# Two activations of the first feed-forward part in a buffer of their own, and the final norm's factors scaled later

## The chip, the cores and the metric

The kernel runs on one NeuronCore of a Trainium2 chip. Its engines run side by side, each through its own list of instructions: TensorE (PE in the profile) multiplies matrices, VectorE (DVE) and ScalarE (ACT) work on elements, GpSimd (POOL) does a few small things, SyncE (SP) issues transfers from memory. The metric is the device time of one execution in microseconds; smaller is better.

## What is computed

A decoder trunk of two layers over 256 tokens with 1,024 features. Layer 0 mixes tokens with a gated recurrence (HGRN2), layer 1 with attention; a SwiGLU feed-forward part follows each mixer, and a last RMSNorm closes the trunk. Cut to what matters here:

```python
for layer in range(2):
    y = rms_norm(h, norm_mix[layer])
    h = h + (hgrn2_mixer if layer == 0 else moba_mixer)(y, ...)
    h = h + swiglu(rms_norm(h, norm_ffn[layer]), ffn_w13[layer], ffn_w2[layer])
return rms_norm(h, final_norm)

def swiglu(h, w13, w2):              # w13: 1024 x 5632, w2: 2816 x 1024
    g, u = jnp.split(h @ w13, 2, axis=-1)
    return (silu(g) * u) @ w2
```

## The kernel before

**Split products.** Every large product is made of three matmuls, since each float32 operand is split into a high part that TensorE takes and a low part that is the rest: high by high, high by low, low by high. ScalarE makes the high part of a weight tile (`whi`, line 412) and VectorE the low part (`wlo`, line 414) out of the tile `raw` that SyncE has fetched. Six buffers of each kind, of 1,024 columns, follow each other round.

**What is stationary and what moves.** In the mixers' projections and in layer 0's feed-forward part the weights are stationary (128 columns) and the 256 tokens of an activation move past them. The tiles are `xh`/`xl` for a normed input and `hh`/`hl` for the 22 hidden pieces j of a feed-forward part. In the second product of layer 1's feed-forward part it is the other way round: the activation `hh`/`hl` is stationary, and 512 columns of weights move. The helper `mm` (line 455) records all of these.

**A feed-forward part** (`swiglu`) first makes the hidden pieces 0 to 3 together. Then it goes in rounds: for j from 4 to 21 it makes piece j (48 matmuls of 256 columns) and after it applies the second product to piece j-4 (layer 0: 24 matmuls of 256 columns; layer 1: 12 of 512). After the rounds come the last four pieces. `hidden` (line 955 on) turns a finished bank into `hh` and `hl`; ring number `j % 7`, each ring with two buffers that take turns.

**Where the tiles lie.** `lay_out` places the tiles of TensorE's operands first, one after the other in each partition: the weights; a gap of 48 floats (192 bytes); the tiles `x`; then the rings `q1`, `k1`, `q2`, `k2` and so on. The rings `q`/`k` serve the recurrence in layer 0's mixer, and `alias` gives the same memory to `hh`/`hl` later: `hh0` lies in `q1`, `hl0` in `k1`, `hh1` in `q2`. All weight tiles begin at a multiple of 512 bytes, and pieces of them too. Counted from there modulo 256, all `x` tiles and the rings from `q2` on lie at 192 bytes. `q1` and `k1` are different: a gap of 64 bytes goes ahead of them, and their tiles are 48 floats longer than what is used. So their first buffers lie at 0 modulo 256 (256 bytes behind a piece of weights, counted modulo 512), and their second ones at 192. By the turns of the rings, `hh0`/`hl0` are in the first buffers for j = 0 and 14 in layer 0 and for j = 7 and 21 in layer 1.

**Order of the work.** TensorE's order is the program's. For the other engines the class `Order` records each operation with a due time and a cost in nanoseconds, and puts it into its engine's list when its inputs are planned to be ready. On the chip each list then runs strictly in turn: an instruction that waits holds up all behind it.

**The final norm's factors.** Behind layer 1's mixer the kernel needs 1/sqrt of the mean square of each token: squares on ScalarE (`sq`, `sqacc`, line 554 on), their sum on VectorE, eight small matmuls against `ones`, a power on GpSimd (`ny`), and two transposes (line 596). At that place ScalarE also issues the transfer of the 1,024 factors of the last norm into `bt` (line 1136), 512 KB with the copies for all partitions, and multiplies them by a constant (line 1137). They are first read at the end, by GpSimd (line 1182).

Of the kernel before, what the change touches and what calls it, by code (L numbers as in the profile page):

```python
# [8 lines left out]
FT = mybir.dt.float32  # L9
FR = mybir.dt.float32r  # L10
I32 = mybir.dt.int32
U8 = mybir.dt.uint8
AF = mybir.ActivationFunctionType
OP = mybir.AluOpType

P = 128
S = 256
D = 1024
# [264 lines left out]
def cv(n, fast=False):  # L283
    return ((n / 2 if fast else n) + 66) / 0.96


def ca(n, ptr=0):
    return n / 1.2 + 93 + 93 * ptr
# [14 lines left out]
def hybrid_trunk(ctx: ExitStack, tc: tile.TileContext, wts, xT, par, gfin, tab, onehot, masks, out):  # L303
    nc = tc.nc
    V, A, G, T = nc.vector, nc.scalar, nc.gpsimd, nc.tensor

    ctx.enter_context(tc.manual_schedule())
    sb = ctx.enter_context(tc.tile_pool(name="sb", bufs=1))
    ps = ctx.enter_context(tc.tile_pool(name="ps", bufs=4, space=bass.MemoryType.PSUM))
    dr = ctx.enter_context(tc.tile_pool(name="dr", bufs=1, space=bass.MemoryType.DRAM))  # L310
    od = Order()
    rings = {}

    def ring(tag, shape, bufs, dt=FT):
        if tag not in rings:
            rings[tag] = Ring(lambda: sb.tile(shape, dt, name=tag, tag=tag, bufs=bufs), bufs)
        return rings[tag]

    def new(tag, shape, bufs=1, dt=FT, held=False):
        return ring(tag, shape, bufs, dt).new(held)  # L320

    def alias(tag, other, shape, dt=FT):

        o = rings[other]
        wide = [P, S + 48] if other in ("q1", "k1") else shape
        rings[tag] = Ring(lambda: sb.tile(wide, dt, name=tag, tag=other, bufs=o.bufs)[:, :shape[1]], o.bufs)
        rings[tag].past = o.past

    def lay_out():


        sb.tile([P, 96], FT, name="lead")
        for t in ("whi", "wlo"):
            ring(t, [P, SUB], NSUB, FR).make()
        sb.tile([P, 48], FT, name="gap")
        for k in range(KT):
            for part in "hl":
                ring(f"x{part}{k}", [P, S], 2, FR).make()
        for part in "qk":

            sb.tile([P, 16], FT, name=f"gap{part}1")
            rings[f"{part}1"] = Ring(lambda part=part: sb.tile([P, S + 48], FT, name=f"{part}1", tag=f"{part}1",
                                                              bufs=2)[:, :S], 2)
            rings[f"{part}1"].make()
            sb.tile([P, 16], FT, name=f"gap{part}2")
        for m in (2, 4, 8, 16, 32, 64):
            for part in "qk":
                ring(f"{part}{m}", [P, S], 2).make()

    def fixed(tag, shape, dt=FT):  # L350
        b = new(tag, shape, 1, dt)
        b.tile = b.ring.make()
        return b
# [4 lines left out]
    def bank(g, held=False):  # L358
        return rings["ps" + g].new(held)

    def main_bank(g):

        b = bank(g, held=True)
        r = b.ring
        od.need(lambda: od.free_at(r))
        b.tile = r.make()
        r.past.append(b)
        return b
# [85 lines left out]
    def mm(o, a, b, start=False, stop=False):  # L454
        T.matmul(o, a, b, start=start, stop=stop, skip_group_check=True)  # L455
# [23 lines left out]
    def mm_w(o, w, x, start=False, stop=False):  # L479
        mm(o, w.hi, x.hi, start=start)  # L480
        od.main(MM)
        mm(o, w.lo, x.hi)
        od.main(MM)
        mm(o, w.hi, x.lo, stop=stop)
        od.main(MM, 1)
        od.pump()
# [34 lines left out]
    for k0, k1 in [(k, k + 1) for k in range(4)] + [(4, 6), (6, 8)]:  # L521
        od.op("S", 60, lambda k0=k0, k1=k1: nc.sync.dma_start(hT[:, k0:k1, :], xT[:, k0:k1, :]),
              writes=hb[k0:k1], nbytes=131072 * (k1 - k0), due=8 * k0 - 6)
    NMK = 2 * P + 64 * 2 * len(LEVELS)
    bt = new("bt", [P, NH * S])
# [146 lines left out]
    for i in range(2):  # L672
        od.op("V", 80, lambda i=i: V.tensor_tensor(le[:, i], gain(5 + i), lbm.tile, op=OP.subtract), reads=[lbm],
              writes=[le], due=12)
# [5 lines left out]
          writes=[oml], due=30)  # L680
# [241 lines left out]
    for k in range(KT):  # L922
# [8 lines left out]
    e = new("be", [P, 384])  # L931
# [4 lines left out]
          reads=[tb], alloc=[tbr], due=80)  # L936
# [3 lines left out]
    for a in range(P // REP):  # L940
# [3 lines left out]
            reads=[scr_b], writes=[bt], nbytes=131072, due=90)  # L944


    def swiglu(layer, x, stats, gu, down):

        hs = {}

        def hidden(j, b):
            gs = new("sgq", [P, S], 3)
            sg = new("u", [P, S], 3)
            due = 6
            od.op("V", cv(S), lambda: V.tensor_tensor(gs.tile, b[:, :S], stats.row.tile, op=OP.mult),  # L955
                  reads=[b, stats.row], alloc=[gs], due=due)
            od.op("A", ca(S), lambda: A.activation(sg.tile, gs.tile, AF.Sigmoid), reads=[gs], alloc=[sg], due=due)  # L957
            od.op("V", cv(S), lambda: V.tensor_tensor(gs.tile, gs.tile, sg.tile, op=OP.mult), reads=[sg], writes=[gs], due=due)
            od.op("V", cv(S), lambda: V.tensor_tensor(sg.tile, b[:, S:], gs.tile, op=OP.mult), reads=[b, gs], writes=[sg],
                  due=due)  # L960
            x = X("h", j % 7)
            hi, lo = x.h, x.l
            od.op("A", ca(S), lambda: A.activation(hi.tile, sg.tile, AF.Copy), reads=[sg], alloc=[hi], due=due + 6)
            od.op("V", cv(S), lambda: V.tensor_tensor(lo.tile, sg.tile, hi.tile.bitcast(FT), op=OP.subtract),
                  reads=[sg, hi], alloc=[lo], due=due + 6)
            hs[j] = x

        bk = [main_bank(gu) for _ in range(4)]
        for k in range(KT - 2):
            w = {}  # L970
            keep["from"] = ws["sub"]
            for j in range(4):
                for half in range(2):
                    w[j, half] = piece("ffn_w13", layer, k, half * DFF + P * j, P)
                    o = bk[j][:, half * S:half * S + S]
                    mm(o, w[j, half].hi, x[k].hi, start=(k == 0 and half == 0))
                    od.main(MM)
                    mm(o, w[j, half].lo, x[k].hi)
                    od.main(MM, .67)
                    od.pump()  # L980
            for j in range(4):
                for half in range(2):
                    mm(bk[j][:, half * S:half * S + S], w[j, half].hi, x[k].lo)
                    od.main(MM, .33)
                od.pump()
            keep["from"] = None
            free_subs(ws["sub"])
        for j in range(4):
            for half in range(2):
                for k in (KT - 2, KT - 1):  # L990
                    mm_w(bk[j][:, half * S:half * S + S], piece("ffn_w13", layer, k, half * DFF + P * j, P), x[k],
                         stop=(k == KT - 1))
            wrote(bk[j])
            hidden(j, bk[j])
            bk[j].held = False
        for j in range(4, FTN):
            b = main_bank(gu)
            for half in range(2):
                for k in range(KT):
                    mm_w(b[:, half * S:half * S + S], piece("ffn_w13", layer, k, half * DFF + P * j, P), x[k],  # L1000
                         start=(k == 0 and half == 0), stop=(k == KT - 1))
            wrote(b)
            hidden(j, b)
            b.held = False
            od.written(stats.row)
            down(j - 4, hs)
        for k in range(KT):
            x[k].free()
        down(FTN - 4, hs, last=True)
# [119 lines left out]
    for k in range(KT):  # L1129
# [4 lines left out]
    gf = new("bt", [P, NH * S])  # L1134
    gf.tile = bt.tile[:, :D]
    od.op("S", 60, lambda: A.dma_start(gf.tile, gfin.to_broadcast([P, D])), writes=[bt], nbytes=524288, due=60)
    od.op("A", ca(D), lambda: A.activation(gf.tile, gf.tile, AF.Copy, scale=-(float(D) ** 0.5) / 2), reads=[bt],
          writes=[gf], due=100)
    ht = new("ii", [P, 2, D])

    def flip_h(tt, half):
# [74 lines left out]
    def down1(k, hs, last=False):  # L1216
        if not acc1:
            acc1[0] = [[main_bank("A") for _ in range(2)] for _ in range(2)]
        ks = range(k, FTN if last else k + 1)
        keep["from"] = ws["sub"]  # L1220
        w = {(kk, nh): piece("ffn_w2", 1, kk, 512 * nh, 512) for kk in ks for nh in range(2)}
        if last:
            od.op("A", 100, lambda: A.activation(warm, ones, AF.Sqrt), due=0)
        for tt in range(2):
            if not last:
                for nh in range(2):
                    mm_x(acc1[0][nh][tt][:, :], hs[k], w[k, nh], tt, start=(k == 0))
                continue
            fin = Final(tt)
            for i, (nh, o, n) in enumerate(FIN):  # L1230
                b = acc1[0][nh][tt]
                for kk in ks:
                    p = w[kk, nh]
                    mm_x(b[:, o:o + n], hs[kk], Piece(p.i, p.c + o, n), tt, stop=(kk == FTN - 1), cost=n / 2.4 + 2.5)
                wrote(b)
                fin.part(i)
            fin.end()
        keep["from"] = None
        free_subs(ws["sub"])
        if not last:  # L1240
            hs[k].free()
# [49 lines left out]
```

## Time and profile before

| What | Value |
|---|---|
| Time, median of 3 runs | 633.11 us (631.64 to 633.42) |
| The profiled execution: its time, its span | 633.35 us, 631.6 us |
| TensorE (PE) busy | 621.1 us, 98% |
| VectorE (DVE), ScalarE (ACT), GpSimd (POOL) busy | 440.2, 364.7, 36.4 us |
| Mean share of the 16 transfer engines over the span | 53.8% for the queue of the weights |
| Mean granted TensorE clock | 0.994 |

The span runs from the first instruction to the last. Busy time of TensorE counts a matmul from its start to its modelled end; neighbours overlap, so that 98% says that it is nearly always at work, not that it is at its best pace. Its pace is read from starts: how many microseconds a known number of matmuls take. [...]

### The profile page before, as it was taken

The numbers are of one execution on the slowest core, as the hardware profiler recorded it, in microseconds if no ns is written. First come the engines' busy times: TensorE is split into PE (matmuls) and PEld (weight loads), VectorE is DVE, ScalarE is ACT, GpSimd is POOL, SyncE is SP. The second block draws the span as 40 slices with busy tenths as digits, with TensorE's granted clock in tenths as the row PEclk, the third lists the DMA queues.
The fourth block names the chain that finished last, engine by engine and source line by source line (L and its number), as shares of the span: only waits on it lengthen the run. The fifth ranks groups of instructions, "written<-read, shape, count | busy, mean of one in ns | idle before, by whom it ended". The sixth has DMA issues, their size and how long they took to land.

```text
span 631.6 us, 12483 instructions
## 1 busy us (share of the span) xinstructions
PE 621.1 (98%) x4868; PEld 597.7 (95%) x4868; DVE 440.2 (70%) x795; ACT 364.7 (58%) x715; POOL 36.4 (6%) x74
## 2 busy tenths in 40 slices
PE   8999999999999999999999999999999999999995
PEld 7899999999999999999998899999999999999994
DVE  6997788767686666666669678866586666666653
ACT  6788888856454444444447566565574444444443
POOL 0131011000300000000001000000100000000003
PEclk9999999999999999999999999999899999999998
DMA  8864444253986566665564665445546666656501
GB/s 307 319 226 132 136 129 137 99 167 101 237 272 189 189 195 199 198 192 188 192 200 122 208 207 168 139 163 167 183 151 201 199 194 195 180 177 186 171 1 67
DMA packets 32135, 111.83 MB, mean 177 GB/s; under 512 B 3835, under 2 KB 4508, under 8 KB 32076
## 3 DMA queue, kind: packets, MB, share of 16 engines
q1 hardware_dynamic: 31052, 108.71, 53.8%
q0 software_dynamic: 448, 1.25, 1.0%
q10 hardware_dynamic: 576, 1.08, 0.6%
q8 instruction: 38, 0.62, 0.4%
q14 instruction: 21, 0.17, 0.1%
HBM read 109.78 MB, written 1.25 MB: 176 GB/s over the span
## 4 chain that ended last, share of the span: by engine, by line
PE 94%; ACT 2%; DMA 2%; DVE 1%; issue 0%; SPq 0%; ACTq 0%
PE psB L455 47%; PE psA L455 47%; DMA bt<-in_final_dram 1%; DMA raw<-in_w_dram 1%; ACT whi L412 1%; PE psB L1098 0%; PE psB L1146 0%; DVE sqacc L559 0%; PE psA L596 0%; ACT xh L539 0%; ACT k L792 0%; DVE raw L1177 0%; ACT sq L1180 0%; ACT raw L1207 0%; DVE wlo L414 0%
## 5 line engine op out<-in xcount | busy, mean ns | idle before, releaser
L414 DVE TENSOR_TENSOR wlo<-raw,whi 128x1024 fp32r<-128x1024 f32 (+1 forms) x206 | 247.9, 1214 | 111.6 <-ACT whi L412 111.0
L412 ACT ACTIVATE whi<-raw 128x1024 fp32r<-128x1024 f32 (+1 forms) x205 | 213.0, 1050 | 150.3 <-issue 66.5
L455 PE MATMUL psB<-xh,whi 128*128 128x256 f32 x608 | 173.4, 288 | 0.0
L455 PE MATMUL psB<-xh,wlo 128*128 128x256 f32 x608 | 168.9, 281 | 0.0
L455 PE MATMUL psB<-xl,whi 128*128 128x256 f32 x608 | 163.4, 280 | 0.0
L455 PE MATMUL psA<-xh,whi 128*128 128x256 f32 x544 | 150.5, 280 | 0.0
L455 PE MATMUL psA<-xh,wlo 128*128 128x256 f32 x544 | 148.8, 277 | 0.0
L455 PE MATMUL psA<-xl,whi 128*128 128x256 f32 x544 | 143.8, 277 | 0.0
L455 PEld LDWEIGHTS psB<-xh,wlo 128*128 128x128 f32 x608 | 115.4, 190 | 0.7
L455 PEld LDWEIGHTS psB<-xh,whi 128*128 128x128 f32 x608 | 115.2, 190 | 0.8
L455 PEld LDWEIGHTS psB<-xl,whi 128*128 128x128 f32 x608 | 112.6, 190 | 0.0
L455 PEld LDWEIGHTS psA<-xh,whi 128*128 128x128 f32 x544 | 102.4, 188 | 0.6 <-issue 0.5
L455 PEld LDWEIGHTS psA<-xh,wlo 128*128 128x128 f32 x544 | 102.2, 188 | 0.0
L455 PEld LDWEIGHTS psA<-xl,whi 128*128 128x128 f32 x544 | 99.2, 188 | 0.0
L455 PE MATMUL psB<-hl,whi 128*128 128x256 f32 x176 | 48.7, 277 | 0.0
L455 PE MATMUL psB<-hh,whi 128*128 128x256 f32 x176 | 48.7, 277 | 0.0
L455 PE MATMUL psB<-hh,wlo 128*128 128x256 f32 x176 | 48.7, 277 | 0.0
L957 ACT ACTIVATE u<-sgq 128x256 f32<-128x256 f32 x44 | 18.1, 410 | 39.3 <-DVE sgq L955 38.6
L455 PE MATMUL psA<-wlo,hh 128*128 128x512 f32 x88 | 34.6, 393 | 0.0
L455 PE MATMUL psA<-whi,hl 128*128 128x512 f32 x88 | 34.5, 392 | 0.0
L455 PE MATMUL psA<-whi,hh 128*128 128x512 f32 x88 | 34.5, 392 | 0.0
L455 PEld LDWEIGHTS psB<-hl,whi 128*128 128x128 f32 x176 | 33.1, 188 | 0.0
(177 smaller groups left out, 791.4 us busy)
## 6 DMA issues: line engine op xcount, KB each, us to landing
raw<-in_w_dram SPq DMA_DIRECT2D x202, 512.0 KB, 4.3
raw<-in_w_dram SPq DMA_DIRECT2D x4, 256.0 KB, 4.7
bt<-scr POOLq DMA_DIRECT2D x8, 128.0 KB, 9.1
hT<-in_x_dram SPq DMA_DIRECT2D x4, 128.0 KB, 4.8
hT<-in_x_dram SPq DMA_DIRECT2D x2, 256.0 KB, 6.3
bt<-in_final_dram ACTq DMA_DIRECT2D x1, 512.0 KB, 5.4
out_dram<-raw ACTq DMA_DIRECT2D x2, 256.0 KB, 2.3
out_dram<-raw SPq DMA_DIRECT2D x2, 256.0 KB, 2.1
```

Source lines behind the costliest of these rows:

```text
L412: od.op("A", ca(n), lambda h=h, r=r, o=o, n=n: A.activation(h[:, :n], r[:, o:o + n], AF.Copy), reads=[r], alloc=[h], due=due)
L414: od.op("V", cv(n), lambda h=h, lo=lo, r=r, o=o, n=n: V.tensor_tensor(lo[:, :n], r[:, o:o + n], h[:, :n].bitcast(FT), op=OP.subtract), rea ...
L455: T.matmul(o, a, b, start=start, stop=stop, skip_group_check=True)
L957: od.op("A", ca(S), lambda: A.activation(sg.tile, gs.tile, AF.Sigmoid), reads=[gs], alloc=[sg], due=due)
```

## The change

The rings `q1` and `k1` become like all the others, so that all buffers of `hh` and `hl` lie at 192 bytes modulo 256. Behind the rings come, after a gap of 64 bytes, two new tiles `eh0` and `el0`, one buffer each, at 0 modulo 256; a gap of 192 bytes follows. In layer 0, the hidden pieces 0 and 11 go into `eh0`/`el0`; all other pieces, and all of layer 1, use the rings. Tiles that are placed after these lie 1,280 bytes (5 x 256) further on. The multiplication of the final norm's factors is recorded no longer beside their transfer but when the second feed-forward product of layer 1 begins.

```diff
     def alias(tag, other, shape, dt=FT):
         o = rings[other]
-        wide = [P, S + 48] if other in ("q1", "k1") else shape
-        rings[tag] = Ring(lambda: sb.tile(wide, dt, name=tag, tag=other, bufs=o.bufs)[:, :shape[1]], o.bufs)
+        rings[tag] = Ring(lambda: sb.tile(shape, dt, name=tag, tag=other, bufs=o.bufs), o.bufs)
...
-        for part in "qk":
-            sb.tile([P, 16], FT, name=f"gap{part}1")
-            rings[f"{part}1"] = Ring(lambda part=part: sb.tile([P, S + 48], FT, name=f"{part}1", tag=f"{part}1",
-                                                              bufs=2)[:, :S], 2)
-            rings[f"{part}1"].make()
-            sb.tile([P, 16], FT, name=f"gap{part}2")
-        for m in (2, 4, 8, 16, 32, 64):
+        for m in (1, 2, 4, 8, 16, 32, 64):
             for part in "qk":
                 ring(f"{part}{m}", [P, S], 2).make()
+        sb.tile([P, 16], FT, name="gape")
+        for part in "hl":
+            ring(f"e{part}0", [P, S], 1, FR).make()
+        sb.tile([P, 48], FT, name="gapf")
...
-            x = X("h", j % 7)
+            x = X("e", 0, 1) if (layer, j) in ((0, 0), (0, 11)) else X("h", j % 7)
...
-    od.op("A", ca(D), lambda: A.activation(gf.tile, gf.tile, AF.Copy, scale=-(float(D) ** 0.5) / 2), reads=[bt],
-          writes=[gf], due=100)
...
     def down1(k, hs, last=False):
         if not acc1:
             acc1[0] = [[main_bank("A") for _ in range(2)] for _ in range(2)]
+            od.op("A", ca(D), lambda: A.activation(gf.tile, gf.tile, AF.Copy, scale=-(float(D) ** 0.5) / 2), reads=[bt],
+                  writes=[gf], due=30)
```

How the instructions stand: line numbers after the change are 2 to 5 lower, and a number behind a name only tells buffers apart. ScalarE's list behind layer 1's mixer, before; `bt` is the final norm's factors, `xh` the high part of the next input, `sq` squares for its norm:

```order
L1136 DMA bt<-in_final_dram 128x1024
L558 ACTIVATE sq<-hT 128x512
L1137 ACTIVATE bt<-bt 128x1024
L539 ACTIVATE xh_6076<-hT,pv 128x256
L539 ACTIVATE xh_6078<-hT,pv 128x256
L558 ACTIVATE sq<-hT 128x512
```

The same place after the change:

```order
L1133 DMA bt<-in_final_dram 128x1024
L555 ACTIVATE sq<-hT 128x512
L536 ACTIVATE xh_6075<-hT,pv 128x256
L536 ACTIVATE xh_6077<-hT,pv 128x256
L555 ACTIVATE sq<-hT 128x512
```

The multiplication of `bt` has left this place; the transfer has stayed, and the rest keeps its order. Where it has gone, in ScalarE's list at the first rounds of layer 1's feed-forward part (`ii` is the transposed residual for the last norm, `u` a sigmoid), after the change:

```order
L1144 ACTIVATE ii<-psB 128x512 x2
L960 ACTIVATE hh_6425<-u 128x256
L1214 ACTIVATE bt<-bt 128x1024
L954 ACTIVATE u<-sgq 128x256
L1144 ACTIVATE ii<-psB 128x512
```

Before, `hh_6426` and `u` were neighbours there; nothing else moves on ScalarE. TensorE's list where piece 0 enters layer 0's second product, before:

```order
L455 MATMUL psA<-xh_2460,wlo 128x256
L455 MATMUL psA<-xl_2478,whi 128x256
L455 MATMUL psB<-hh_2693,whi 128x256
L455 MATMUL psB<-hh_2693,wlo 128x256
L455 MATMUL psB<-hl_2712,whi 128x256
```

After:

```order
L452 MATMUL psA<-xh_2460,wlo 128x256
L452 MATMUL psA<-xl_2478,whi 128x256
L452 MATMUL psB<-eh_2693,whi 128x256
L452 MATMUL psB<-eh_2693,wlo 128x256
L452 MATMUL psB<-el_2712,whi 128x256
```

Only the operand's place has changed. The same holds for piece 11, and no list of any other engine differs but by these names.

## Rows read from the trace of the kernel before

**Rows 1.** The page: span, granted clock in 40 slices, chain by engine, VectorE's costliest group.
```profile
span 631.6 us, 12483 instructions
PEclk9999999999999999999999999999899999999998
PE 94%; ACT 2%; DMA 2%; DVE 1%; issue 0%; SPq 0%; ACTq 0%
...
L414 DVE TENSOR_TENSOR wlo<-raw,whi 128x1024 fp32r<-128x1024 f32 (+1 forms) x206 | 247.9, 1214 | 111.6 <-ACT whi L412 111.0
```
**Rows 2.** Chain of waits behind layer 1's mixer: start, us, what, how many.
```profile
433.68 5.37 DMA bt<-in_final_dram
...
440.03 0.89 ACT xh L539 x2
...
442.88 0.69 DVE sqacc L559
...
443.71 1.02 PE psA L455 x8
444.73 3.63 PE psB L455 x22
448.36 0.43 PE psA L596 x2
448.79 17.11 PE psB L455 x142
```
**Rows 3.** Timeline of ScalarE there: start, us, instruction, [idle before <- releaser].
```profile
439.06 1.06 ACT L1137 ACTIVATE bt<-bt 128x1024 f32<-128x1024 f32 x1 [2.85 <-DMA bt<-in_final_dram]
```
**Rows 4.** Timeline of VectorE there: the last two residual adds.
```profile
436.93 1.28 DVE L611 TENSOR_TENSOR hT<-psA,hT 128x512 f32<-128x512 f32 x2
```
**Rows 5.** Timeline of TensorE there: the last matmul ahead of the eight sums, and these.
```profile
442.16 0.28 PE L455 MATMUL psB<-xh,wlo 128*128 128x256 f32 x1
443.71 1.02 PE L455 MATMUL psA<-ones,sqacc 128*128 128x1 f32 x8 [1.27 <-DVE sqacc L559]
```
**Rows 6.** Stretches: length, busy us of PE, PEld, DVE, ACT, POOL, granted clock, DMA share, GB/s.
```profile
160.90:164.80 3.90, 3.90 (x36) 3.90 (x35) 2.70 (x4) 0.83 (x1) 2.63 (x3) 1.00 1.01 234
...
446.08:449.50 3.42, 3.42 (x19) 3.42 (x18) 1.23 (x3) 0.68 (x2) 1.60 (x1) 0.50 0.87 269
```
**Rows 7.** Chain of waits in layer 0's feed-forward part, columns as in rows 2.
```profile
161.10 0.79 PE psB L455 x8
161.89 2.70 PE psA L455 x22
164.58 0.22 PE psB L596 x2
164.80 16.73 PE psA L455 x142
181.53 2.87 PE psB L455 x24
...
192.58 5.44 PE psA L455 x48
...
295.94 2.86 PE psB L455 x24
```
**Rows 8.** Chain of waits in layer 1's feed-forward part, columns as in rows 2.
```profile
477.29 2.75 PE psA L455 x12
...
518.36 2.75 PE psA L455 x12
...
529.31 5.65 PE psB L455 x48
534.96 2.77 PE psA L455 x12
...
610.74 13.74 PE psA L455 x60
```
**Rows 9.** Timeline of GpSimd in layer 0: the power between sums and transposes.
```profile
162.17 1.63 POOL L591 TENSOR_TENSOR ny<-nv,mhalf 128x2 f32<-128x2 f32 x1 [1.31 <-DVE nv L588]
```

## The prediction

> **What bounds the kernel now.** I read the page first, then TensorE's waits, the chain of waits, and the timelines around the two places where the change acts. On the page the chain is TensorE's for 94% [rows 1], so the time is the number of matmuls times their pace, plus the few gaps. Three things stand out.
>
> First, one gap late in the program. TensorE's matmul at 442.16 is followed by the eight sums only at 443.71, and the row names VectorE's sum of squares as what it waited for [rows 5]. The chain goes back from there through VectorE and ScalarE to the transfer of the final norm's factors, 5.37 us from issue to landing [rows 2]. ScalarE stood 2.85 us before its multiplication of `bt` and then took 1.06 us for it [rows 3], and the splits and squares behind it in its list began only at 440.03 [rows 2]. What these read was there at 438.21, when VectorE's two residual adds ended (436.93 + 1.28), and half of it after the first of the two, at about 437.57 [rows 4].
>
> Second, the granted clock. [...] Before it fell TensorE had stood idle for 1.27 us and then done eight matmuls of one column. The same eight sums in layer 0, without a gap before them, had a granted clock of 1.00 around them [rows 6].
>
> Third, TensorE's pace has levels that no clock explains. Matmuls of 256 columns go at 113 ns in one stretch (5.44 us for 48) and at 118 ns in another (16.73 for 142) [rows 7], and the clock was full up to the start of the slower one [rows 6] and in the slices after it [rows 1]. A level lasts until something resets it. In layer 0 the slower one ends with the 24 matmuls on piece 0 (2.87 us, so 120 ns each), after which the faster one holds; piece 14 again takes 2.86 us and leaves the faster one in force [rows 7]. In layer 1 the rounds are short up to 518.36: five rounds in 518.36 - 477.29 = 41.07 us, 8.21 each. From the round after j-4 = 7 on they are long: nine in 610.74 - 534.96 = 75.78 us, 8.42 each, with 5.65 us for the 48 [rows 8]. Pieces 0 and 14 in layer 0 and 7 in layer 1 are those whose `hh0`/`hl0` lie in the first buffers, at 0 modulo 256; pieces in the second buffers, at 192, changed nothing. So I read this: a piece at 0 modulo 256 resets the pace; as a moving operand it sets the faster level, as a stationary one the slower.
>
> **The change part by part.** All sums are against the profiled execution, 633.35 us, which is 0.24 us over the median of the three runs (they spread over 1.8 us).
>
> *The multiplication moved away from ScalarE's list.* Without it the splits can begin at about 437.6 instead of 440.03, some 2.4 us sooner, and the sum of squares that ended at 443.57 (442.88 + 0.69) [rows 2] ends at about 441.2. TensorE comes to the eight sums about 442.3, so nothing is waited for, with 1 us to spare. Worth: 443.71 - 442.16 = 1.55, less an ordinary step of 0.11 = 1.44 us [rows 5]. The weight splits behind on both engines move forward by as much, so they are not late next.
>
> *The clock then stays up.* The price of the dip comes from a twin: layer 0 runs the same sequence after its sums (22 matmuls, two transposes, 142 matmuls) from 161.89 to 181.53, 19.64 us [rows 7]; in layer 1 it takes from 444.73 to 448.79 + 17.11 = 465.90, 21.17 us [rows 2]. The difference is 1.53 us. From above it is bounded by half of the 3.42 us at half clock, 1.71 [rows 6]. From below it is 0, if the clock falls all the same. I take 1.53, since the twin has the same work without a gap.
>
> *The multiplication where it now stands.* 1.06 us [rows 3] on ScalarE between two rounds of layer 1, its transfer long landed. Behind it wait a sigmoid and a copy of the transposed residual, for pieces that TensorE needs only four rounds (4 x 8.21 us) later. I price it at 0; if that cover were gone, at 1.06.
>
> *Layer 1 without a piece at 0 modulo 256.* Piece 7 now lies like its neighbours, whose rounds stay at 8.21. The ten rounds from 526.57 (518.36 + 8.21) to 610.74 save 8.42 - 8.21 each: 2.06 us [rows 8]. The bounds are 0 (something else resets the pace) and 2.1.
>
> *Layer 0.* Piece 0 still lies at 0 modulo 256, now in `eh0`/`el0`, and should still lift the pace; piece 11 takes piece 14's part, 24 x (120 - 113) ns = 0.16 us paid there as before. `el0` lies 512 bytes away from where `hl0` lay, modulo 1,024; since successive pieces of weights alternate by 512 bytes too, the 24 matmuls see the same relations. Net 0. The single buffer adds no wait: piece 0 is used up in round 4, and piece 11 is made seven rounds later.
>
> *Everything behind the new tiles* moves by 1,280 bytes, a multiple of 256, and `k1` in layer 0's mixer moves from 0 to 192 in its first buffer. The small matmuls of the mixers stand between runs of 256-column matmuls and each may leave another level behind. One such run is short, but the 142 matmuls in each layer before the first round are 142 x 4.5 ns = 0.64 us each. I put 0 in the sum and +-1.3 us in the range.
>
> Sum: 1.44 + 1.53 + 2.06 = 5.03; 633.35 - 5.03 = 628.3, and 628.1 against the median. I say **628.2**.
>
> [...] The trace shows 120 ns at one place of the operand and 113 at another for the same shapes [rows 7]. [...]
>
> **The rivals.**
>
> *The place of an operand isn't what sets the level* in layer 1, and the rounds go to 8.42 all the same. For it: one switch only was seen there, at piece 7, while piece 21 came too late to show anything. Time: 633.35 - 2.97 = 630.4. [...]
>
> *TensorE stays on the slower level (this one ends slower than before).* If `eh0`/`el0` do not lift the pace, the 1,320 matmuls from piece 0 to the end of layer 0's part (17 x 48 for pieces 5 to 21, 21 x 24 for the second product) cost 4.5 ns more each, 5.9 us: 634.2, about as before. If layer 1 begins its rounds on that level too, its gain of 2.06 is lost and the six rounds from 477.29 to 526.57 lose 0.21 each: 637.5. It decides from 5.03 us / 4.5 ns, some 1,120 slower matmuls. Against it: both times that a piece at 0 modulo 256 moved past the weights, the faster level followed [rows 7].
>
> *The wait comes back one step later.* The sums feed a power on GpSimd of 1.63 us [rows 9], and then the two transposes. In layer 0 it ended at 163.80, 0.78 us before these [rows 7]. In layer 1 its input stands in VectorE's list behind a weight split of 1.21 us [rows 1], which can now fall just when the sums end. TensorE could then wait up to 1.21 - 0.78 = 0.4 us, and the clock could fall after it, 1.53 more: 630.2; with a full split in the way, 631.0.
>
> *The clock falls anyway*, since the eight sums alone make TensorE idle enough. Against it: layer 0's [rows 6]. Time: 633.35 - 1.44 - 2.06 = 629.9.
>
> *More than forecast*: both runs of 142 matmuls come to the faster level, 1.3 us: 627.0.
>
> **How the numbers follow.** Forecast 0.49; levels not set by place 0.12; slower level in layer 0 alone 0.07, in both 0.07; the later wait 0.08; the clock falls anyway 0.07; more than forecast 0.10. About 0.3%, 1.9 us, can be told from no change: faster means under 631.2, slower over 635.0. Faster: the forecast, the first rival, the clock, the extra gain and half of the later wait, 0.82. Same: layer 0 alone and the other half, 0.11. Slower: 0.07. The range 626.0 to 631.2 takes in the forecast with its +-1.3 us (and below that 0.9, half the spread of the three runs) and all the cases but the slower level and half of the later wait, which leaves out 0.18.
>
> **What would show it.** Right: no wait of TensorE on the sum of squares at 442; a granted clock of 1.00 there up to the end of the matmuls; rounds of 8.21 us in layer 1 up to the last; 24 matmuls at 120 ns for pieces 0 and 11 in layer 0, with 5.44 us for 48 after both. Wrong: 5.65 us for 48 in layer 1 (place is not the cause), or 118 ns in layer 0 after piece 0 (the new tiles don't lift the pace), or a wait at line 596's transposes, or a dip of the clock that stays.

## The result, and the profile after

The changed kernel took 628.25 us (median of 4 executions, 628.15 to 629.05) beside 632.67 for the kernel before (4 executions, three of them those of the table ahead): a ratio of 0.9934, with a 95% interval from 0.9919 to 0.995. Its profiled execution took 628.23 us. Timed again later, it took 628.28 us.

| | before | after |
|---|---|---|
| profiled execution, us | 633.35 | 628.23 |
| its span, us | 631.6 | 626.4 |
| TensorE's wait for the sum of squares behind layer 1's mixer, us | 1.27 | none |
| a round of layer 1 behind piece 7, us | 8.42 | 8.21 |

The page after, against [rows 1]: span, and granted clock in the 40 slices (in tenths of full speed; 9 is 90% or more).

```profile
span 626.4 us, 12483 instructions
...
PEclk9999999999999999999999999999999999999999
```

The dip of the clock is gone. The next rows are the place of [rows 2 to 5] after the change, one timeline for each engine (start, us, instruction, in brackets the idle time before it and what ended it). ScalarE, with the splits that had begun at 440.03:

```profile
437.56 0.91 ACT L536 ACTIVATE xh<-hT,pv 128x256 fp32r<-128x256 f32 x2 [1.44 <-DVE hT L608]
```

VectorE, the last sum of squares, and TensorE, the sums over it:

```profile
440.43 0.68 DVE L556 TENSOR_TENSOR sqacc<-sqacc,sq 128x512 f32<-128x512 f32 x1
```
```profile
442.20 0.95 PE L452 MATMUL psA<-ones,sqacc 128*128 128x1 f32 x8
```

The splits now follow VectorE's addition, not the multiplication of `bt`. The last sum of squares ends at 440.43 + 0.68 = 441.11, and TensorE comes to the eight sums 1.09 us later, with no idle time in the row. The power on GpSimd and the two transposes behind it:

```profile
443.81 1.60 POOL L588 TENSOR_TENSOR ny<-nv,mhalf 128x2 f32<-128x2 f32 x1 [97.31 <-DVE nv L585]
```
```profile
445.68 0.38 PE L593 MATMUL psA<-ident,ny 128*128 128x128 f32 x2
```

The power ends at 445.41, 0.27 us before the transposes: they don't wait, but the room is small. The clock there, in stretches (length, busy us of PE, PEld, DVE, ACT, POOL, granted clock, DMA share, GB/s), against the 0.50 in [rows 6]:

```profile
442.20:445.70 3.50, 3.50 (x33) 3.50 (x32) 2.66 (x4) 0.96 (x2) 1.60 (x1) 1.00 0.57 177
445.70:462.00 16.30, 16.30 (x141) 16.30 (x140) 10.97 (x18) 10.68 (x15) 0.00 (x0) 1.00 0.67 221
```

The chain of waits there (start, us, what, how many), against [rows 2]; in a chain a step begins where the one before it ends:

```profile
435.10 7.26 PE psB L452 x64
442.36 0.79 PE psA L452 x8
443.15 2.70 PE psB L452 x22
...
446.06 16.73 PE psB L452 x142
```

The 64 matmuls ahead of the sums go at 113 ns, the 142 behind at 118. The chain around piece 11 in layer 0, and in rounds of layer 1, against [rows 7, 8]:

```profile
271.36 2.86 PE psB L452 x24
274.22 5.46 PE psA L452 x48
279.68 2.72 PE psB L452 x24
```
```profile
523.48 2.75 PE psA L452 x12
526.22 5.47 PE psB L452 x48
...
605.61 13.75 PE psA L452 x60
```

Piece 11 pays 2.86 us for its own 24 matmuls, as piece 14 did, and the next 24 take 2.72. In layer 1 the ten rounds from 523.48 to 605.61 take 8.21 us each.

### The profile page after: what moved, and what is told of

It is laid out like the page before. It is cut to its first block, busy times and chain, and to the rows that moved or that the text cites. A ratio compares the mean times of both kernels' runs of the same rounds, so it can differ in the third digit from the quotient of the medians.

```text
span 626.4 us, 12483 instructions
## 1 busy us (share of the span) xinstructions
PE 617.1 (99%) x4868; PEld 594.2 (95%) x4868; DVE 440.2 (70%) x795; ACT 364.7 (58%) x715; POOL 36.7 (6%) x74
## 4 chain that ended last, share of the span: by engine, by line
PE 95%; ACT 2%; DMA 1%; DVE 1%; SPq 0%; issue 0%; ACTq 0%
PE psA L452 47%; PE psB L452 47%; DMA raw<-in_w_dram 1%; ACT whi L409 0%; PE psB L1095 0%; PE psB L1141 0%; SPq L398 0%; SPq L519 0%; DVE wlo L411 0%; ACT k L789 0%; PE psA L593 0%; DVE raw L1172 0%; ACT sq L1175 0%; ACT raw L1202 0%; ACT pm L871 0%
## 5 line engine op out<-in xcount | busy, mean ns | idle before, releaser
L452 PE MATMUL psB<-xh,whi 128*128 128x256 f32 x608 | 171.6, 285 | 0.0
L452 PE MATMUL psB<-xh,wlo 128*128 128x256 f32 x608 | 167.1, 278 | 0.0
L452 PE MATMUL psB<-hl,whi 128*128 128x256 f32 x160 | 44.2, 276 | 0.0
L452 PE MATMUL psB<-hh,whi 128*128 128x256 f32 x160 | 44.2, 276 | 0.0
L452 PE MATMUL psB<-hh,wlo 128*128 128x256 f32 x160 | 44.2, 276 | 0.0
L452 PEld LDWEIGHTS psB<-hh,whi 128*128 128x128 f32 x160 | 30.0, 188 | 0.0
```

## The experiments

Where a range is given, the kernel was timed in several executions beside the kernel before; a time without one is of a single execution. The kernel before itself took 632.3 us in the median beside the first four kernels (25 executions, 630.97 to 634.57) and 632.85 beside the next four (9 executions, 631.32 to 633.47). The first four ran on another chip than all that follow, so a difference of medians between the two groups holds the difference of the chips too (0.55 us in the kernel before); the ratios, which carry an interval, compare each kernel with the kernel before beside it.

**Each part alone.** The multiplication moved, the buffers left as before:

```diff
-    od.op("A", ca(D), lambda: A.activation(gf.tile, gf.tile, AF.Copy, scale=-(float(D) ** 0.5) / 2), reads=[bt],
-          writes=[gf], due=100)
...
             acc1[0] = [[main_bank("A") for _ in range(2)] for _ in range(2)]
+            od.op("A", ca(D), lambda: A.activation(gf.tile, gf.tile, AF.Copy, scale=-(float(D) ** 0.5) / 2), reads=[bt],
+                  writes=[gf], due=30)
```

> The kernel before with the multiplication of the final norm's factors moved alone; buffers as before. Theory (the wait and the clock dip come from that multiplication, the long rounds of layer 1 from a piece at 0 modulo 256): 3.0 us less than before in the profiled execution, about 630.3; no wait on the sum of squares, granted clock 1.00 up to the last matmuls, but rounds of 8.42 us in layer 1 from the round that applies piece 7. Rival (the long rounds are an after-effect of the gap or of the clock): rounds of 8.21 us to the end, 628.3.

Measured: 630.67 us (630.27 to 631.19, 8 executions), a ratio of 0.9968 (0.9957 to 0.998); span 628.5. TensorE no longer waits for the sum of squares, and the rounds of layer 1 turn long behind piece 7 as before. Chain of waits of this kernel:

```profile
518.02 5.47 PE psB L455 x48
523.49 2.73 PE psA L455 x12
526.22 5.65 PE psB L455 x48
531.88 2.77 PE psA L455 x12
```

Now the buffers alone, the multiplication back beside its transfer:

```diff
+    od.op("A", ca(D), lambda: A.activation(gf.tile, gf.tile, AF.Copy, scale=-(float(D) ** 0.5) / 2), reads=[bt],
+          writes=[gf], due=100)
...
             acc1[0] = [[main_bank("A") for _ in range(2)] for _ in range(2)]
-            od.op("A", ca(D), lambda: A.activation(gf.tile, gf.tile, AF.Copy, scale=-(float(D) ** 0.5) / 2), reads=[bt],
-                  writes=[gf], due=30)
```

> The changed kernel with the multiplication put back where it was before. Theory: the wait of 1.3 us on the sum of squares and the dip of the clock come back, rounds in layer 1 stay at 8.21 us; 3.0 us over the changed kernel, 631.2. Rival (the clock doesn't hang on the gap): the gap of 1.4 us comes back alone and the clock stays at 1.00, 629.7.

Measured: 630.76 us (629.62 to 631.58, 9 executions), ratio 0.9968 (0.9957 to 0.998); span 627.8. From the end of its 142 matmuls (448.10 + 16.11, the chain below) to the end of the span it takes 163.6 us, as in the changed kernel (626.4 - 462.79), so the rounds of layer 1 stay short, 8.21 us as there. TensorE's waits in the profiled execution (what is waited for, us in total, times, longest):

```profile
PE psA L452 <- DVE sqacc L556: 0.8, 1, 0.8
PE psA L593 <- POOL ny L588: 0.6, 1, 0.6
```

The waits moved: the sum of squares costs 0.8 us instead of 1.27, the transposes wait another 0.6 for the power, and the clock didn't fall. So a wait at this place doesn't always bring the dip. It does in some executions, it seems: in four of the nine the mean clock was 0.994 or 0.995, against 0.998 in the profiled one here and 0.994 in that of the kernel before. The run of 142 matmuls behind it took this form in the chain:

```profile
448.10 16.11 PE psB L452 x142
```

That is the faster level, where the changed kernel has 16.73 us: 0.6 us that the wait gives back. In the medians each part alone gains 1.5 to 1.6 us, and both together 4.0 to 4.6. By the ratios each part alone gains 0.32%, that is 2.0 us (+-0.7), and both together 0.64 to 0.66%, some 4.1 us: within the noise the parts add up.

**The place of the two new tiles.** At 192 modulo 256, like all the others:

```diff
-        sb.tile([P, 16], FT, name="gape")
         for part in "hl":
             ring(f"e{part}0", [P, S], 1, FR).make()
-        sb.tile([P, 48], FT, name="gapf")
+        sb.tile([P, 64], FT, name="gapf")
```

> The changed kernel with its two new tiles at 192 modulo 256 like all the other activations; all later tiles stay where they are. Theory (only a piece at 0 modulo 256 lifts the pace): after piece 0 in layer 0 the matmuls stay at 118 ns, 48 in 5.65 us, to the end of that part; 1,320 x 4.5 ns less the two slow pieces' 0.3 us, so 5.6 us over the changed kernel, 633.8; layer 1's rounds may come out at either level, 633.8 to 637. Rival (the place doesn't matter, the matmuls of the second product reset the pace themselves): as the changed kernel, 628.2, with 113 ns after piece 0.

Measured: 633.95 us (633.32 to 634.53, 10 executions), ratio 1.0025 (1.0013 to 1.0036). Piece 0 in layer 0 now leaves the pace where it was, in the chain:

```profile
181.35 2.83 PE psB L451 x24
184.17 5.65 PE psA L451 x48
...
451.41 16.73 PE psB L451 x142
482.28 5.47 PE psB L451 x48
```

118 ns per matmul holds from there to the end of layer 0, and the whole gain of the change is lost and a little more. Layer 1's rounds are not touched (5.47 for 48 throughout), though the run of 142 ahead of them is at the slower level (last two rows). The same instructions in the same order, with nothing but two addresses moved, cost 5.7 us.

**Piece 7 of layer 1 back at 0 modulo 256**, in the new tiles:

```diff
-            x = X("e", 0, 1) if (layer, j) in ((0, 0), (0, 11)) else X("h", j % 7)
+            x = X("e", 0, 1) if (layer, j) in ((0, 0), (0, 11), (1, 7)) else X("h", j % 7)
```

> The changed kernel with piece 7 of layer 1 in the new tiles too, where it is the stationary operand at 0 modulo 256. Theory: the rounds of layer 1 go from 8.21 to 8.42 us from the round that applies piece 7 on, ten rounds, 2.05 us over the changed kernel, 630.3. Rival (the long rounds before came from something else, such as the ring's longer tiles): rounds of 8.21 us to the end, 628.2.

Measured: 630.56 us (630.12 to 630.79, 6 executions), ratio 0.9963 (0.995 to 0.9976), span 628.3. The round behind piece 7 again goes from one level to the other:

```profile
517.85 5.47 PE psB L452 x48
523.32 2.73 PE psA L452 x12
526.05 5.66 PE psB L452 x48
531.71 2.77 PE psA L452 x12
```

One piece at 0 modulo 256 as stationary operand is enough: it costs 1.9 us of span, 2.3 us in the medians, 1.7 by the ratios.

**The changed kernel once more, with no edit**, beside the next three:

> The changed kernel once more, beside the three kernels below and many executions of the kernel before. 628.2 by every theory; what is asked is the median of before over more executions (633.1 if the clock dips in most of them as in the profiled one, 631.5 to 632.3 if in few), and so whether the gain is 5.0 us or nearer 4.

Measured: 628.28 us (628.02 to 629.32, 5 executions), ratio 0.9936 (0.9922 to 0.9951). Against the two medians of before the gain is 4.0 and 4.6 us.

**Another way to reset the pace, sooner.** A second copy of the fifth input tile lies in `eh0`/`el0` in both feed-forward parts and is read in the first pass alone, and all hidden pieces lie in the rings. So the run of 142 matmuls ahead of the first round is lifted too, and no piece pays 120 ns.

```diff
+        if i == 2 and "e" in x:
+            split_x({4: x["e"]}, 4, g, due + 20)
...
     x1 = {k: X("x", k) for k in range(KT)}
+    x1["e"] = X("e", 0, 1)
...
-            x = X("e", 0, 1) if (layer, j) in ((0, 0), (0, 11)) else X("h", j % 7)
+            x = X("h", j % 7)
...
+            xk = x["e"] if k == 4 else x[k]
...
-                    mm(o, w[j, half].hi, x[k].hi, start=(k == 0 and half == 0))
+                    mm(o, w[j, half].hi, xk.hi, start=(k == 0 and half == 0))
...
-                    mm(bk[j][:, half * S:half * S + S], w[j, half].hi, x[k].lo)
+                    mm(bk[j][:, half * S:half * S + S], w[j, half].hi, xk.lo)
...
+        x["e"].free()
...
     x3 = {k: X("x", k) for k in range(KT)}
+    x3["e"] = X("e", 0, 1)
```

> The changed kernel with the piece at 0 modulo 256 taken earlier: in both feed-forward parts the fifth tile of the normed input has a copy in the new tiles, used only in the first pass over the weights; pieces 0 and 11 of layer 0 go back to the rings. Theory (24 matmuls that move a tile at 0 past the weights leave the faster level behind): in layer 0 about 120 and in layer 1 about 110 matmuls ahead of the rounds go from 118 to 113 ns, 1.0 us, and the two slow pieces' 0.3 us are saved: 626.9. Rival (a level is set by the second product's start alone): the 1.0 us isn't had and layer 0 stays at 118 ns, 633.

Measured: 627.38 us (626.89 to 627.84, 5 executions), ratio 0.9919 (0.9905 to 0.9933), span 625.5. It is 0.90 us faster than the changed kernel beside it, and its slowest execution is below the fastest of that one. Its chain behind layer 1's mixer, where the changed kernel has 442.36 for the sums and 462.79 for the end of the long run:

```profile
441.84 0.79 PE psA L452 x8
442.63 3.17 PE psB L452 x26
445.80 0.22 PE psA L593 x2
446.01 15.82 PE psB L452 x138
461.84 0.44 PE psB L1147 x4
```

From the sums to the row behind the long run it takes 461.84 - 441.84 = 20.00 us against 20.43. The two slow pieces of layer 0 save some 0.15 each. It beats both kernels.

**One reset instead of two.** Only piece 0 in the new tiles:

```diff
-            x = X("e", 0, 1) if (layer, j) in ((0, 0), (0, 11)) else X("h", j % 7)
+            x = X("e", 0, 1) if (layer, j) == (0, 0) else X("h", j % 7)
```

> The changed kernel without piece 11 in the new tiles. Theory (the level holds until something else resets it): 113 ns to the end of layer 0's part, and 24 x 6.7 ns = 0.16 us less, 628.1. Rival (the level decays and piece 11 renews it): 118 ns from somewhere on, up to 2.6 us more, 630.8.

Measured: 628.41 us (627.95 to 628.75, 5 executions), ratio 0.9935 (0.9922 to 0.9949). The faster level holds to the end of layer 0 without piece 11:

```profile
271.25 2.72 PE psB L452 x24
273.98 5.44 PE psA L452 x48
```

The span is 626.2 us, against 626.4. So nothing in layer 0's rounds lowers the pace again, and piece 11 at 0 modulo 256 costs its 0.16 us for nothing; too little to be seen in the times.

**A wait put where the old one was.** Eleven copies of a tile onto itself on ScalarE, behind the transfer of `bt`; they change no value:

```diff
+    od.op("A", 60, lambda: [A.activation(e.tile, e.tile, AF.Copy) for _ in range(11)], reads=[e], writes=[e], due=0)
```

> The changed kernel with eleven copies of 384 columns onto themselves on ScalarE at the place where the multiplication was, so that TensorE waits at the eight sums for about 1.9 us (11 x 0.41 - 2.66) with everything else as in the changed kernel. Theory (a gap of that length, with the one-column matmuls behind it, makes the clock fall): granted clock 0.50 for some 3.4 us behind it; 628.2 + 1.9 + 1.5 = 631.6, or 630.1 in executions where it doesn't fall. Rival (the dip in the kernel before had another cause): clock 1.00 throughout, 630.1 to 630.7 always.

Measured: 636.41 us (635.47 to 637.57, 4 executions), ratio 1.0063 (1.0041 to 1.0085). The wait came out longer than planned, for two reasons. The copies followed each other every 0.56 us and took 6.09 together (the 0.41 of the expectation is the cost that the kernel's own plan, `ca`, gives 384 columns). And they stood ahead of `sq` as well: VectorE waited 5.82 us for it, and the residual add that the last splits read stood behind in VectorE's list. The timelines of VectorE and of TensorE, and the stretch at the lower clock:

```profile
442.29 0.69 DVE L556 TENSOR_TENSOR sqacc<-sqacc,sq 128x512 f32<-128x512 f32 x1 [5.82 <-ACT sq L555]
```
```profile
447.31 1.84 PE L452 MATMUL psA<-ones,sqacc 128*128 128x1 f32 x8 [4.81 <-DVE sqacc L556]
```
```profile
444.94:455.18 10.24, 7.87 (x37) 7.90 (x38) 5.75 (x9) 4.93 (x9) 1.60 (x1) 0.50 0.44 154
```

So the last sum of squares ended later by all of the copies' time (at 447.17, against 441.11 in the changed kernel), and only the 1.09 us by which it had come ahead of TensorE was room, where the expectation took off 2.66. The idle time alone is worth 4.81 - 0.11 = 4.7 of the 8.1 us; the rest is the work at a granted clock of 0.50, where the 22 matmuls behind the sums took 4.90 us in the chain, instead of 2.70. All four executions show a mean clock of 0.990 or 0.991, so it seems to have fallen behind this gap each time. That a gap of TensorE can bring the clock down at this place is shown by this; how long the gap must be is not.

**The kernel before in another execution**, since the dip hung on a single one:

> The kernel before once more, for a second profile of it. If most of its executions have no dip of the clock (granted clock 0.996 to 0.999 in 28 of 34 timed ones, but 0.994 in the one profiled first): wait of some 1.3 us on the sum of squares, clock 1.00 behind it, a second wait of about 0.6 us at the transposes as in e2_buffer_only, rounds of 8.42 us in layer 1 from the round that applies piece 7; 632.3. If the dip belongs to the gap: 0.50 for 3.4 us again, 633.4.

Measured: 631.29 us, span 629.5, at the low end of before. The wait is shorter and the clock doesn't fall. (By the list of executions 29 of the 34 were at 0.996 or more, not 28.) TensorE's timeline, the stretch behind it, the chain, and TensorE's wait at the transposes:

```profile
443.07 1.02 PE L455 MATMUL psA<-ones,sqacc 128*128 128x1 f32 x8 [0.86 <-DVE sqacc L559]
```
```profile
443.60:447.20 3.60, 3.20 (x27) 2.99 (x26) 3.08 (x4) 1.38 (x2) 1.57 (x1) 1.00 0.46 154
```
```profile
447.28 0.43 PE psA L596 x2
447.71 16.12 PE psB L455 x142
```
```profile
PE psA L596 <- POOL ny L591: 0.5, 1, 0.5
```

The transposes wait 0.5 us for the power, and the 142 matmuls behind them run at the faster level.

**Other places.** The new tiles at 64 and at 128 modulo 256 (the two gaps 32 and 32, or 48 and 16, instead of 16 and 48):

```diff
-        sb.tile([P, 16], FT, name="gape")
+        sb.tile([P, 32], FT, name="gape")
...
-        sb.tile([P, 48], FT, name="gapf")
+        sb.tile([P, 32], FT, name="gapf")
```

> The changed kernel with its two new tiles at 64 modulo 256 instead of 0, all else in place. If only a place of 0 lifts the pace: as e3_at192, 118 ns to the end of layer 0's part, 633.9. If any place that puts these matmuls at another pace than 113 or 118 ns does it: 113 ns after piece 0, 628.2.

> The changed kernel with its two new tiles at 128 modulo 256. As for 64: 633.9 if only 0 lifts the pace, 628.2 if another place does too.

Measured: 628.93 us and 630.54. At 64 the tiles lift the pace just as well; at 128 piece 0 lifts it and piece 11 lowers it again. Each was seen in one execution. Chains around piece 0 and piece 11 at 64, then at 128:

```profile
182.25 2.83 PE psB L452 x24
185.07 5.45 PE psA L452 x48
...
272.12 2.83 PE psB L452 x24
274.95 5.45 PE psA L452 x48
```
```profile
181.62 2.85 PE psB L452 x24
184.47 5.47 PE psA L452 x48
...
271.54 2.85 PE psB L452 x24
274.39 5.65 PE psA L452 x48
```

So place 0 is not the only one that resets the pace, and at 128 the level flips.

**All activations at 0 modulo 256:**

```diff
-        sb.tile([P, 48], FT, name="gap")
+        sb.tile([P, 64], FT, name="gap")
...
-        sb.tile([P, 16], FT, name="gape")
```

> The changed kernel with a gap of 64 floats instead of 48 between the weights and the activations, so that all the tiles of activations lie at 0 modulo 256. Theory (a moving operand at 0 goes at 120 ns always): nearly 4,000 matmuls of 256 columns, most of them now at 113.3 ns and some 1,000 at 118, go at 120; about 20 us over the changed kernel, 648. Rival (the 120 ns come from the change of place, not from the place): 113 or 118 ns as now, 628 to 634.

Measured: 648.48 us, span 646.7. Nearly all matmuls of 256 columns go at 120 ns, in both layers:

```profile
187.48 5.76 PE psA L451 x48
...
492.74 5.75 PE psB L451 x48
```

20 us of this kernel hang on where the activations begin, with the same instructions and a mean clock of 0.997.

## Why the prediction was right, step by step

**The wait.** The sum of squares was forecast to end at 441.2 and TensorE to come to the sums at 442.3; measured were 441.11 and 442.20. The step held as worked out: the splits waited for `bt`'s multiplication only because it stood ahead of them in ScalarE's list.

**The clock.** It stays at 1.00. Wait and clock together were put at 1.44 + 1.53 = 2.97 us for the profiled execution. From the end of the matmuls ahead of the sums to the end of the 142, before took 465.90 - 442.44 = 23.46 us [rows 2, 5], and after takes 446.06 + 16.73 - 442.36 = 20.43: 3.03. Layer 0's twin was the right measure: from the end of the sums to the end of the 142, after takes 462.79 - 443.15 = 19.64 us, the twin's time.

**What was mis-sized.** The gain in a usual execution. In the other execution of before the same stretch takes 463.83 - 442.21 = 21.62 us, so there the two terms are worth 1.19: no dip, a shorter wait, and 0.6 us given back by the faster level of the 142. In the medians the first two experiments give 1.6 us (the multiplication moved, against before) and 2.5 (the changed kernel against the buffers alone) for them, by the ratios 2.0 both times. A mean clock of 0.995 or less, as in the profiled execution, was shown by 9 of 43 timed executions of the two kernels with the multiplication at its old place (before 5 of 34, the buffers alone 4 of 9), and by none of 43 of the six without it there (the kernel with the copies left out). So, as far as the mean clock marks it, the dip hangs on that place but comes in about one execution of five, and the gain against the medians is 4.0 to 4.6 us instead of 5.0. The time itself came out because the profiled execution, with its wait and dip, was priced against a stretch without them. The gain is smaller because that execution lies 0.5 to 1.05 us over those medians.

**The multiplication's new place** cost nothing that the chain shows: it is TensorE's from the sums at 442.36 through all of layer 1's rounds, to 619.36.

**Layer 1's rounds.** Forecast 2.06 us; spans give 2.1 (the multiplication alone, against after) and 1.9 (piece 7 put back). The first has the old buffers, the second differs from the changed kernel by piece 7 alone, and both have the long rounds: the cause is piece 7's place. The rival by which the place doesn't set the level falls. And with all activations at 0 modulo 256 this kernel takes 20 us more (648.48 us beside 628.28).

**Layer 0.** Net 0, as forecast; the rival that put the loss of the faster level at 5.9 us (634.2) was made real by the tiles at 192: 633.95. The worse case, in which layer 1 begins at the slower level too (637.5), didn't come: its rounds stayed at 5.47 us for 48. But the reading behind it was too narrow in two places. That only 0 modulo 256 resets the pace is wrong (with piece 0 at 64 the 48 behind it take 5.45 us), and piece 11 was taken as needed to hold the level, which it isn't (5.44 us for 48 without it).

**The later wait** at the transposes didn't come; by the timeline 0.27 us were left of it. The 0.78 us of layer 0 in the prediction was read from the chain; by the timeline its transposes begin at 164.42, 0.62 after the power. In the two profiled executions that wait for the sum of squares without a dip (0.8 and 0.9 us), the later wait came on top, with 0.6 and 0.5.

**The runs of 142 matmuls** stayed at the slower level in both layers (16.73 us), the middle of the +-1.3 us. The slower level begins at the eight sums, not in the mixers: the 64 matmuls ahead of them go at 113 ns in layer 1, and in layer 0 of the kernel before 16 take 1.81 us ahead of them (from 157.76) and 11 take 1.29 right behind (from 161.95). What brings the faster level back ahead of the first round is open. In the two executions whose transposes waited 0.5 and 0.6 us it was there behind them (142 in 16.12 and 16.11 us). With the copies it was there too (142 in 16.51 us, the first 0.71 of them at a granted clock of 0.50) though the transposes hadn't waited, only stood in the stretch at 0.50; in the profiled execution of before, with the same 0.71 us at 0.50, it wasn't (142 in 17.11 us, 16 of them in 1.88 from 450.18).

## What to carry to other kernels

Here a multiplication that waited 2.85 us for a transfer held up all that stood behind it in its engine's list, and the splits began at 440.03 us instead of 437.56: record such an operation where its result is wanted, not where its data is asked for. Read TensorE's pace per matmul for each stretch of the chain; where one shape has two paces at the same clock (here 113 and 118 ns at 1.00), compare the places of its operands before anything else, and remember that a level may have been set a thousand matmuls earlier (with piece 0 alone in the new tiles it held, by the span, for some 1,300). Before a dip or a wait from one profile is priced as a gain, look whether other executions have it (here 9 of 43 showed the lower mean clock).

## What the hardware showed that was not expected

For pairs of a 128x128 weight load and a matmul of 256 columns in this kernel, at a granted clock of 1.00, there are three paces: 113 ns (5.44 us for 48), 118 (16.73 for 142) and 120 (2.87 for 24). Two of them, 113 and 118, are states that last: in layer 0 some 1,300 matmuls, 113 with piece 0 alone in the new tiles (e7_once, by its span), 118 with the tiles at 192 (e3_at192). The weights stayed where they are in all these kernels.

| place of the activations, modulo 256 bytes | their own pace, ns | level that they leave behind | read from |
|---|---|---|---|
| 192 | 113 or 118, as found | the one they found (but see below) | 24 in 2.72 us (changed kernel), in 2.83 (e3_at192) |
| 0 as moving operand | 120 | 113 | 24 in 2.86, then in 2.72 (changed kernel, piece 11) |
| 0 as stationary operand (layer 1) | - | 118 | 48 in 5.47, then in 5.66 (e4_piece7) |
| 64 as moving operand | 118 | 113 | 24 in 2.83, then 48 in 5.45 (e10_at64) |
| 128 as moving operand | 119 | 113 if 118 was found, 118 if 113 was found (each once) | 24 in 2.85, then 48 in 5.47 and in 5.65 (e11_at128) |

The place is not all that sets the level. The eight sums end the faster one in both layers: in the changed kernel 64 go at 113 ns ahead of them in layer 1, 142 at 118 behind; in layer 0 of the kernel before 16 take 1.81 us ahead of them and 11 take 1.29 behind. And layer 1 comes back to it with every activation at 192: with the new tiles there, the 142 matmuls take 16.73 us and the rounds behind them 5.47 for 48. Even in such a round the first six of the 48 start 117 to 122 ns after one another, and only the next ones 113 (the changed kernel, from 526.06).

Nor is it the moving operand's place alone. In layer 1's second product pieces of weights move, from multiples of 512 bytes, past an activation at 192, and the long rounds behind piece 7 stay long for all that (5.65 us for 48 and 2.77 for 12 to the end, in the kernel before). Whether the distance between the two operands decides, no run shows, since the weights were never moved. Why the memory or the engine does this, no run here tells.

In the profiled executions the granted clock didn't fall behind idle times of 0.8 and 0.9 us, fell for 3.42 us in one execution with 1.27 us [rows 5, 6], and for 10.24 us in the one with 4.81. At 0.50 the matmuls of 256 columns began 213 ns after one another (the kernel before, from 446.24 to 448.16), at 1.00 behind the dip 118.

Copies on ScalarE of a 128x384 tile onto itself took 0.56 us from start to start.
